# Attention with bias: eight chunks of k or q transposed in one block, and the emission model's cost for it

## The chip, the core and the metric

The kernel runs on one core of a Trainium2 chip. Its engines work from queues of their own, in the order in which the program emits the instructions: TensorE (PE; its weight loads are listed as PEld), VectorE (DVE), ScalarE (ACT), GpSimd (POOL) and SyncE (SP); the last two mostly issue DMAs here. The metric is the device time of one execution in microseconds, lower is better.

## What is computed

Softmax attention with an additive bias that is shared by all batches and heads, for 4 x 8 = 32 heads, 1024 positions and a head dimension of 64, with inputs and outputs in float32:

```python
scale = 1.0 / np.sqrt(head_dim)
scores = scale * np.matmul(q, k.transpose(0, 1, 3, 2))
scores = scores + bias
scores_max = np.max(scores, axis=-1, keepdims=True)
attn = np.exp(scores - scores_max) / (np.sum(np.exp(scores - scores_max), axis=-1, keepdims=True) + 1e-8)
return np.matmul(attn, v)
```

## The kernel before

**Tiling.** Two heads form a pair (16 pairs). The 1024 positions of queries and of keys are cut into 8 chunks of 128. A *slot* is one head with one chunk of queries against all 1024 keys: 256 slots. The scores of a slot, transposed (keys on partitions), fill one of three *places* `pl` in PSUM, each of 128 x 1024 float32 (two banks). The slots are ordered in two groups of pairs (7 and 9). Slots of one chunk of queries follow each other in a place, head after head: only the first of such a chain writes the bias by matmuls (L223), and each later one adds the scores of its head and takes away those of the head before, in one matmul over 64 + 64 rows. So a pair has the operands `ko` and `qo` (both its heads, the first of `qo` negated) for its second head, and `ke` and `qe` for its first, which join it to the second head of the pair before.

**The work of a slot.** Two halves of four matmuls make its *fill* (`fill`, L228; the matmuls are at L226). ScalarE takes the exponential of the place into a tile `E` (L240), of which there are 13. For some slots of place 2, VectorE computes the exponential instead, by a chain of six steps (`d_steps`, L249, lines L257 to L277, tiles `dy`, `df`, `dt`, `de`); which slots these are is decided while the program is emitted, by how much work VectorE has. Then eight matmuls multiply the exponentials by V, with a column of ones for the sum (`av`, L285, matmuls at L294), into a PSUM tile `po` that holds up to seven slots; VectorE divides and copies it out (`evac`, L302 and L304), SyncE stores it.

**Getting k and q ready.** GpSimd's DMAs load k and q of a pair as bf16 with positions on partitions. TensorE transposes them by chunks into a PSUM tile `px` (`transposes`, L164; L173). A chunk takes two transposes, one for each head of the pair, each from 128 x 64 to 64 x 128, placed at its own half of the array's columns by `tile_position`. So eight chunks take 16 instructions on L173. VectorE copies `px` into `ko` or `qo` (`copy_out`, L177, lines L181 and L183). SyncE's DMAs, or VectorE or GpSimd for the first pairs, copy halves of that into `ke` and `qe` (`doubles`, L487; `copy`, L513). `px` and `po` share two PSUM buffers, `xa` and `xb`.

**The order.** The whole program is emitted by hand, in the order that a small model finds while it emits (from about L362 to L796): it keeps a time for each engine (`t_pe`, `t_act`, `t_dve`, ...) and, step by step, emits the candidate that can start first. It runs once, when the program is built; on the chip each engine then follows that fixed order and waits on semaphores. The model's durations are constants in ns: `FILL` 452 for a fill, `AVG` 247 or `AV` 264 for a slot's product with V, `EXP` 906 for an exponential on ScalarE, `TR` 60 for a chunk's transposes, `L_PE`, `L_ACT`, `L_DVE` for the way of a result from an engine to the next.

`pe_cands` (L552) lists what TensorE could do next: a fill for each place (priority 0), a product with V (priority 1), and the next *piece* of transposes, all eight chunks of a pair's k or q, or 3 or 5 of them for the q of the first pairs (priority 2, or 0.5 when the first slot that needs it is nine or fewer ahead). There are 32 such pieces. A piece may start only if few exponentials wait for their product (`lag < 4`), or its first use is less than eight slots ahead.

Before the change a piece is two candidates, one after the other: `begin` emits the first half of its chunks, `end` the rest and queues the copy-out. `half_done` holds the piece that is begun, with its buffer; the second half is free of the condition on `lag`. Between the two other candidates may be emitted, or none.

`pe_pick` (L710) chooses. If a fill can start now, it is taken, unless an urgent candidate fits ahead of the moment at which ScalarE runs out of filled places (`act_free`, L523, less `FILL` and `L_PE`). If no fill can start, another candidate is taken if it ends before a limit worked out from the same moment:

```python
limit = max(min(r), act_free() - FILL - L_PE - MARGIN)
ok = [x for x in others if x[0] + x[1] <= limit]
```

Of the kernel before, what the change touches and what calls it, by code (L numbers as in the profile page):

```python
# [16 lines left out]
def kernel(  # L17
# [143 lines left out]
    def linked(pr):  # L161
        return pr + 1 < NP

    def transposes(pr, which, c0, n, tag, px=None, at=0, to=None):  # L164
        if px is None:
            px = ps_x.tile([P, n, P], BF, tag=tag, name="px")
        for c in range(at, to or n):
            if (pr, which, c0) in raws:
                nc.tensor.transpose(px[:, c, :], raws[pr, which, c0][:, c].rearrange("p t d -> p (t d)"), ident[:])
                continue  # L170

            for t in range(2):
                nc.tensor.transpose(px[t * D:(t + 1) * D, c, :], lands[pr, which][:, t, c + c0 * (pr > 0), :], ident[:],  # L173
                                    tile_position=(0, t * D))
        return px
# [141 lines left out]
    with tc.manual_schedule():  # L317
# [68 lines left out]
        t_pe, t_act, t_dve, t_pool = 9300.0, 9900.0, 9600.0, 12800  # L386
# [3 lines left out]
        x_free = {"xa": T0, "xb": T0}  # L390
# [16 lines left out]
        next_fill, next_act = 1, 1  # L407
# [3 lines left out]
        dve_q = []  # L411

        b_tag, closed = [], []
        TR = 60
        LAG, AVG = 7, 247
        half_done = []
        free_lands, loads, loads_v = set(), list(range(EARLY, NP)), []
        sp_q, t_sp = [], T0
        AHEAD, SLACK = 60, 300
# [112 lines left out]
        def fill_ready(s):  # L532
            p = before[s]
            t = 0.0
            if p is not None:
                if p in used:
                    t = used[p]
                elif p in filled and p not in dslots:
                    t = act_free(p) + L_ACT
                else:  # L540
                    return None
            for key in keys(s):
                if get(key) is None:
                    return None
                t = max(t, get(key))
            if slots[s][3]:
                if slots[s][1] not in bias_at:
                    return None
                t = max(t, bias_at[slots[s][1]])
            return t  # L550

        def pe_cands():  # L552

            out = []
            for x in range(3):
                if not queue[x] or queue[x][0] > next_fill + WINDOW:
                    continue
                s = queue[x][0]
                r = fill_ready(s)
                if r is not None and (before[s] is None or before[s] in used):  # L560
                    cost = FILL + BIAS * bool(slots[s][3] and s > 1)

                    def do(t, s=s, x=x, cost=cost):
                        nonlocal next_fill
                        fill(s)
                        filled[s] = t + cost + L_PE
                        queue[x].pop(0)
                        next_fill = min([y[0] for y in queue.values() if y], default=NS)
                        if may_d[s] and backlog(t) < ROOM and len(open_d) < 3:
                            dslots.add(s)  # L570
                            avq.remove(s)
                            start_d(s)
                        else:
                            acts.append(s)
                    out.append((max(t_pe, r), cost, do, 0, s))


            todo = []
            if avq:
                group = [s for s in avq[:1] if round_of[s] == round_of[avq[0]]]  # L580
                have = [s for s in group if s in e_at]
                lag = len([s for s in avq[:NE] if s in e_at])
                if len(have) < len(group):
                    group = have if lag >= LAG and have[:1] == avq[:1] else []
                if avq[0] >= NS - 3:
                    group = [s for s in avq[:1] if s in e_at]
                if group and all(slots[s][2] // 2 in v_at for s in group):
                    todo.append((max(max(e_at[s], v_at[slots[s][2] // 2]) for s in group), group))
            if dav:
                todo.append((dav[0][0], [dav[0][1]]))  # L590
            if todo:
                r, group = min(todo)
                b = len(closed)
                if b_tag:
                    tag = b_tag[0]
                    group = group[:7 - len(bank[b][1])]
                else:
                    f, tag = min((x_free[y], y) for y in x_free)
                    r = max(r, f)
                cost = AVG * len(group) if len(group) > 1 else AV  # L600
                if r < 1e11:
                    def do(t, group=group, b=b, tag=tag, cost=cost):
                        b_tag[:] = [tag]
                        x_free[tag] = 1e12
                        av(group, b, tag)
                        for s in group:
                            if s in dslots:
                                dav.pop(0)
                            else:
                                avq.remove(s)  # L610
                            av_done[s] = t + cost
                        next_v(t)
                        n = len(bank[b][1])
                        if n == 7 or n == 6 and not (dav and dav[0][0] < t + cost + 600) or len(av_done) in (NS - 1, NS):
                            closed.append(b)
                            b_tag.clear()
                            close(b, tag, t + cost + L_PE)
                    out.append((max(t_pe, r), cost, do, 1, 0))
            if pieces:
                pr, which, c0, n = pieces[0]  # L620
                need = need_at[pr, which, c0]
                ring = pr + linked(pr) - RING
                lag = len([s for s in avq[:NE] if s in e_at])
                if ((pr, which, c0) in raw_at and next_fill >= need - AHEAD and (ring < 0 or last_slot[ring] < next_fill)
                        and (lag < 4 or need - next_fill < 8 or half_done)):
                    f, tag = half_done[0] if half_done else min((x_free[y], y) for y in x_free)
                    r = max(f, raw_at[pr, which, c0])
                    to = n if half_done else (n + 1) // 2
                    cost = (n // 2 if half_done else to) * TR
                    urgent = need - next_fill < 12  # L630
                    if r < 1e11:
                        def begin(t, pr=pr, which=which, c0=c0, n=n, tag=tag, to=to):
                            px = transposes(pr, which, c0, n, tag, to=to)
                            x_free[tag] = 1e12
                            half_done[:] = [(t, tag), px, to]

                        def end(t, pr=pr, which=which, c0=c0, n=n, tag=tag, cost=cost):
                            pieces.pop(0)
                            px = transposes(pr, which, c0, n, tag, px=half_done[1], at=half_done[2])
                            half_done.clear()  # L640
                            if pr < EARLY and which == 0 and c0 + n == NCH:
                                freed(pr, t)

                            def run(t2):
                                copy_out(pr, which, c0, n, px)
                                done = t2 + 60 * n + (180 if which else 300)
                                x_free[tag] = done + L_DVE
                                if which:
                                    ready["ko", pr] = done + L_DVE
                                else:  # L650
                                    ready["qo", pr, c0] = done + L_DVE
                                doubles(pr, which, c0, n, done, urgent)
                            dve_q.append((t + cost + L_PE, 0 if urgent else 2, 60 * n + (180 if which else 300), run))
                        out.append((max(t_pe, r), cost, end if half_done else begin, 2 if next_fill < need - 9 else 0.5, 0))
            return out

        def pool(at, cost=0):
# [94 lines left out]
        while next_fill < NS or next_act < len(acts) or avq or dav or dve_q or sp_q:  # L752
            c = []
            if next_act < len(acts):
# [4 lines left out]
                if next_act < NE or acts[next_act - NE] in av_done:  # L759
                    r = max(t_act, filled[s], av_done[acts[next_act - NE]] if next_act >= NE else 0)  # L760
# [13 lines left out]
            t, who = min(c)  # L774
# [14 lines left out]
            else:  # L789
                t_pe = t + p[1]  # L790
# [31 lines left out]
```

## Time and profile before

| | |
|---|---|
| median of 3 runs | 238.88 us (238.15 to 239.96) |
| the profiled execution | 238.87 us, its span 236.8 us |
| TensorE busy / weight loads | 227.0 us (96%) / 211.0 us (89%) |
| ScalarE busy | 222.9 us (94%), 237 exponentials |
| VectorE busy | 197.8 us (84%), 20 exponentials by its chain |
| GpSimd busy | 50.1 us (21%) |
| transposes on L173 | 490, from 10.8 to 141.8 us |
| granted TensorE clock | 0.998 |

Matmuls are pipelined: an instruction is listed for longer than the distance to the next (219 ns for one of a fill, of which eight start within 0.45 us), so busy shares of TensorE overstate how full it is; the distance from the start of one group to that of the next says more. The same holds, less strongly, for ScalarE: an exponential is listed with 1.07 us. The time outside the span (2.07 us) is part of the device time. In rows of the timeline the columns are start and length in us, engine, line, operation, output and input with shapes, the number of instructions merged into the row, and in brackets the idle time before it with what ended it.

### The profile page before, as it was taken

What the parts mean: (1) busy time and instruction counts of PE and PEld (TensorE: products, weight loads), DVE (VectorE), ACT (ScalarE), POOL (GpSimd) and SP (SyncE); (2) the same over time, 40 slices, a digit from 0 to 9 for tenths busy, and PEclk for the clock granted to TensorE, in tenths of its full rate; (3) what the DMA queues carried; (4) which work ended last, traced back from release to release, by engine and by line L of the source; (5) the groups of instructions that cost most, each with busy time, mean ns of one, the idle gap of its engine ahead of it and who ended that gap; (6) DMA issues with size and microseconds to landing.
All of it is one profiled execution on the core that took longest, in us unless ns stands there. A gap on an engine that the chain in (4) does not pass through costs nothing.

```text
span 236.8 us, 10752 instructions
## 1 busy us (share of the span) xinstructions
PE 227.0 (96%) x4743; PEld 211.0 (89%) x4743; DVE 197.8 (84%) x287; ACT 222.9 (94%) x241; POOL 50.1 (21%) x72
## 2 busy tenths in 40 slices
PE   7989999999999999999999999999999999999992
PEld 2879988899989999999999889999999999999981
DVE  2575585889989999989889988998999999899961
ACT  4699998999999999999999999999999999999993
POOL 8844417556403202206131000000000000000000
PEclk9999999999999999999999999999999999999999
DMA  6999999999995948596989452111111111211212
GB/s 210 205 204 214 225 226 210 203 193 204 200 208 122 155 113 156 118 217 97 159 187 183 114 136 64 36 42 42 42 43 44 39 44 47 55 50 49 67 42 61
DMA packets 55358, 29.76 MB, mean 126 GB/s; under 512 B 30800, under 2 KB 51664, under 8 KB 55312
## 3 DMA queue, kind: packets, MB, share of 16 engines
q0 software_dynamic: 30336, 14.06, 47.2%
q1 hardware_dynamic: 24832, 14.50, 23.7%
q8 instruction: 37, 0.61, 1.1%
q10 hardware_dynamic: 144, 0.52, 0.8%
q14 instruction: 9, 0.07, 0.1%
HBM read 29.36 MB, written 8.39 MB: 159 GB/s over the span
## 4 chain that ended last, share of the span: by engine, by line
PE 69%; ACT 16%; issue 7%; DMA 4%; POOL 3%; ACTq 1%; DVE 0%; POOLq 0%
PE pl L226 39%; PE po L294 20%; ACT E L240 16%; PE px L173 7%; DMA q<-in_q_dram 4%; PE pl L223 2%; ACTq L817 1%; POOL k L130 1%; POOL braw L336 0%; POOL qz L332 0%; POOL qs L333 0%; POOL q L138 0%; POOL v L145 0%; POOL ident masks.py:199 0%; DVE ob L304 0%
## 5 line engine op out<-in xcount | busy, mean ns | idle before, releaser
L240 ACT ACTIVATE E<-pl 128x1024 bf16<-128x1024 f32 (+1 forms) x237 | 219.8, 1068 | 6.0 <-PE pl L226 4.9
L294 PE MATMUL po<-vall,E 128*128 128x65 bf16 x1888 | 92.3, 194 | 1.9 <-ACT E L240 1.0
L294 PEld LDWEIGHTS <-E 128*128 128x128 bf16 x1888 | 77.6, 98 | 2.8 <-ACT E L240 1.4
L226 PE MATMUL pl<-qo,ko 128*128 128x128 bf16 x1024 | 77.3, 219 | 0.9 <-ACT E L240 0.2
L226 PEld LDWEIGHTS <-ko 128*128 128x128 bf16 x1160 | 69.0, 98 | 5.3 <-issue 1.0
L226 PE MATMUL pl<-qe,ke 128*128 128x128 bf16 x888 | 66.3, 219 | 1.6 <-DVE qe L194 0.6
L226 PEld LDWEIGHTS <-ke 128*128 128x128 bf16 x888 | 52.6, 98 | 5.1 <-issue 1.0
L257 DVE TENSOR_SCALAR dy<-pl 128x1024 int32<-128x1024 f32 x20 | 24.4, 1221 | 3.7 <-PE pl L226 3.5
L304 DVE TENSOR_TENSOR ob<-po,rs 128x448 f32<-128x448 f32 (+3 forms) x40 | 23.4, 585 | 1.5
L277 DVE SCALAR_TENSOR_TENSOR de<-dy,dt 128x1024 uint16<-128x1024 int32 x20 | 24.4, 1218 | 0.0
L266 DVE SCALAR_TENSOR_TENSOR dt<-df 128x1024 f32<-128x1024 f32 x20 | 24.3, 1217 | 0.0
L272 DVE SCALAR_TENSOR_TENSOR dt<-df,dt 128x1024 f32<-128x1024 f32 x20 | 24.3, 1217 | 0.0
L269 DVE SCALAR_TENSOR_TENSOR df<-dt,df 128x1024 f32<-128x1024 f32 x20 | 24.3, 1217 | 0.1
L138 POOL DMA_DIRECT2D q<-in_q_dram x16 | 11.5, 719 | 42.9 <-PE pl L226 33.0
L149 POOL DMA_DIRECT2D vall<-in_v_dram x18 | 16.2, 907 | 11.7 <-PE pl L226 8.7
L181 DVE COPY ko<-px 128x1024 bf16<-128x1024 bf16 (+1 forms) x16 | 10.8, 673 | 8.5 <-PE px L173 8.0
L302 DVE RECIPROCAL rs<-po 128x7 f32<-128x7 f32 (+3 forms) x40 | 7.9, 197 | 11.8 <-PE po L294 11.4
L183 DVE TENSOR_SCALAR qo<-px,sgn 128x1024 bf16<-128x1024 bf16 (+2 forms) x18 | 12.4, 690 | 5.0 <-PE px L173 4.9
L262 DVE TENSOR_SCALAR df<-dy 128x1024 f32<-128x1024 uint16 x20 | 13.7, 690 | 0.0
L223 PE MATMUL pl<-ident,braw 128*128 128x128 bf16 x136 | 11.7, 228 | 0.3 <-issue 0.2
L130 POOL DMA_DIRECT2D k<-in_k_dram x15 | 10.7, 714 | 3.2 <-PE px L173 1.8
L173 PE MATMUL px<-ident,q 128*64 128x128 bf16 x240 | 11.0, 223 | 0.1
(50 smaller groups left out, 105.9 us busy)
## 6 DMA issues: line engine op xcount, KB each, us to landing
k<-in_k_dram POOLq DMA_DIRECT2D x15, 256.0 KB, 9.6
q<-in_q_dram POOLq DMA_DIRECT2D x14, 256.0 KB, 9.4
out_dram<-ob SPq DMA_DIRECT2D x50, 64.0 KB, 1.8
out_dram<-ob SPq DMA_DIRECT2D x31, 96.0 KB, 3.5
ke<-ko SPq DMA_DIRECT2D x22, 128.0 KB, 5.6
vall<-in_v_dram POOLq DMA_DIRECT2D x18, 128.0 KB, 7.8
qe<-q SPq DMA_DIRECT2D x17, 128.0 KB, 4.2
out_dram<-ob SPq DMA_DIRECT2D x63, 32.0 KB, 1.6
```

The lines of the kernel that those rows point to most:

```text
L149: nc.gpsimd.dma_start(out=vall[:, (2 * pr + t) % VR, :, :D], in_=vf[pr, :, t])
L173: nc.tensor.transpose(px[t * D:(t + 1) * D, c, :], lands[pr, which][:, t, c + c0 * (pr > 0), :], ident[:], tile_position=(0, t * D))
L223: nc.tensor.matmul(to, braw[:, c, :].rearrange("p (kp kc) -> p kc kp", kc=NCH)[:, kc, :], ident8[:], start=i == 0, stop=False, skip_group_ ...
L226: nc.tensor.matmul(to, kk[:, kc, :], qq[:, c, :], start=False, stop=True, skip_group_check=True)
L240: nc.scalar.activation(e[:, i:i + n].rearrange("p b x -> p (b x)"), places[slots[s][0]][:, i:i + n].rearrange("p b x -> p (b x)"), ACTF.Ex ...
L257: w.tensor_scalar(t["y"][:], places[slots[s][0]].rearrange("p b x -> p (b x)"), scale * LOG2E * 65536.0, 127.0 * 65536.0, op0=ALU.mult, op ...
L266: w.scalar_tensor_tensor(t["t"][:], t["f"][:], -G, t["f"][:], op0=ALU.add, op1=ALU.mult)
L269: w.scalar_tensor_tensor(t["f"][:], t["t"][:], Q, t["f"][:], op0=ALU.mult, op1=ALU.add)
L272: w.scalar_tensor_tensor(t["t"][:], t["f"][:], V, t["t"][:], op0=ALU.add, op1=ALU.mult)
L277: w.scalar_tensor_tensor(etile[s].bitcast(U16).rearrange("p c q -> p (c q)"), t["y"][:], 1.0 / 512.0, t["t"][:], op0=ALU.mult, op1=ALU.add)
L294: nc.tensor.matmul(po[:, j + i, :], etile[s][:, kc, :], vall[:, slots[s][2] % VR, kc, :], start=j + i + kc == 0, stop=kc == NCH - 1, skip_ ...
L304: nc.vector.tensor_tensor(ob[:, :n, :], po[:, :n, :D], rs[:, :n, :].to_broadcast([P, n, D]), op=ALU.mult)
```

## The change

The argument range of `transposes` goes; all chunks of a piece are emitted by one call. `begin` and `end` become one candidate, `do`, so nothing is emitted between the chunks of a piece, and `half_done` and the exception that it made from the condition on `lag` go with it. The modelled cost of a piece of n chunks becomes n x 56 + 190 ns; before, it was 60 ns for each chunk of a half. The copy-out is queued at the modelled end of the block, as before. All else in the model and in the emitted work is as it was; as the model's times change, the order and the choice of the slots that VectorE takes are found anew.

```diff
@@ -161,10 +161,10 @@
     def linked(pr):
         return pr + 1 < NP
 
-    def transposes(pr, which, c0, n, tag, px=None, at=0, to=None):
+    def transposes(pr, which, c0, n, tag, px=None):
         if px is None:
             px = ps_x.tile([P, n, P], BF, tag=tag, name="px")
-        for c in range(at, to or n):
+        for c in range(n):
             if (pr, which, c0) in raws:
                 nc.tensor.transpose(px[:, c, :], raws[pr, which, c0][:, c].rearrange("p t d -> p (t d)"), ident[:])
                 continue
@@ -411,9 +411,8 @@
         dve_q = []
 
         b_tag, closed = [], []
-        TR = 60
+        TR, SWITCH = 56, 190
         LAG, AVG = 7, 247
-        half_done = []
         free_lands, loads, loads_v = set(), list(range(EARLY, NP)), []
         sp_q, t_sp = [], T0
         AHEAD, SLACK = 60, 300
@@ -622,22 +621,16 @@
                 ring = pr + linked(pr) - RING
                 lag = len([s for s in avq[:NE] if s in e_at])
                 if ((pr, which, c0) in raw_at and next_fill >= need - AHEAD and (ring < 0 or last_slot[ring] < next_fill)
-                        and (lag < 4 or need - next_fill < 8 or half_done)):
-                    f, tag = half_done[0] if half_done else min((x_free[y], y) for y in x_free)
+                        and (lag < 4 or need - next_fill < 8)):
+                    f, tag = min((x_free[y], y) for y in x_free)
                     r = max(f, raw_at[pr, which, c0])
-                    to = n if half_done else (n + 1) // 2
-                    cost = (n // 2 if half_done else to) * TR
+                    cost = n * TR + SWITCH
                     urgent = need - next_fill < 12
                     if r < 1e11:
-                        def begin(t, pr=pr, which=which, c0=c0, n=n, tag=tag, to=to):
-                            px = transposes(pr, which, c0, n, tag, to=to)
+                        def do(t, pr=pr, which=which, c0=c0, n=n, tag=tag, cost=cost):
                             x_free[tag] = 1e12
-                            half_done[:] = [(t, tag), px, to]
-
-                        def end(t, pr=pr, which=which, c0=c0, n=n, tag=tag, cost=cost):
                             pieces.pop(0)
-                            px = transposes(pr, which, c0, n, tag, px=half_done[1], at=half_done[2])
-                            half_done.clear()
+                            px = transposes(pr, which, c0, n, tag)
                             if pr < EARLY and which == 0 and c0 + n == NCH:
                                 freed(pr, t)
 
@@ -651,7 +644,7 @@
                                     ready["qo", pr, c0] = done + L_DVE
                                 doubles(pr, which, c0, n, done, urgent)
                             dve_q.append((t + cost + L_PE, 0 if urgent else 2, 60 * n + (180 if which else 300), run))
-                        out.append((max(t_pe, r), cost, end if half_done else begin, 2 if next_fill < need - 9 else 0.5, 0))
+                        out.append((max(t_pe, r), cost, do, 2 if next_fill < need - 9 else 0.5, 0))
             return out
 
         def pool(at, cost=0):
```

## The prediction

> **What bounds the kernel now.** I read the chain of waits first, then the waits, ScalarE's timeline, the windows by stage and TensorE's timeline around the transposes.
>
> ```profile
> PE 69%; ACT 16%; issue 7%; DMA 4%; POOL 3%; ACTq 1%; DVE 0%; POOLq 0%
> PE pl L226 39%; PE po L294 20%; ACT E L240 16%; PE px L173 7%; DMA q<-in_q_dram 4%; PE pl L223 2%; ACTq L817 1%; POOL k L130 1%; POOL braw L336 0%; POOL qz L332 0%; POOL qs L333 0%; POOL q L138 0%; POOL v L145 0%; POOL ident masks.py:199 0%; DVE ob L304 0%
> ```
>
> The chain runs through TensorE, with 7% of the span in the transposes (L173). It does not say whether ScalarE has slack, so its timeline comes next: a row is a run of exponentials without a gap over about 0.15 us, and the bracket tells the gap before it.
>
> ```profile
> 22.73 2.85 ACT L240 ACTIVATE E<-pl 128x1024 bf16<-128x1024 f32 x3 [0.18 <-PE pl L226]
> 26.04 11.11 ACT L240 ACTIVATE E<-pl 128x1024 bf16<-128x1024 f32 x12 [0.46 <-PE pl L226]
> ...
> 40.97 2.85 ACT L240 ACTIVATE E<-pl 128x1024 bf16<-128x1024 f32 x3 [0.76 <-PE pl L226]
> 44.04 3.78 ACT L240 ACTIVATE E<-pl 128x1024 bf16<-128x1024 f32 x4 [0.21 <-PE pl L226]
> ...
> 88.68 44.80 ACT L240 ACTIVATE E<-pl 128x1024 bf16<-128x1024 f32 x47 [0.16 <-PE pl L226]
> 133.82 52.02 ACT L240 ACTIVATE E<-pl 128x1024 bf16<-128x1024 f32 x56 [0.34 <-PE pl L226]
> 186.16 46.85 ACT L240 ACTIVATE E<-pl 128x1024 bf16<-128x1024 f32 x51 [0.32 <-PE pl L226]
> ```
>
> The last row gives ScalarE's own pace: (46.85 - 1.07) / 50 = 0.916 us per exponential (one takes 1.07 us, the next begins before it ends). At 88.68 it is (44.80 - 1.07) / 46 = 0.951: small delays that no bracket shows. From 9.12 to 133.82 lie 129 exponentials, one of half size; at 0.916 they need 117.7 us and took 124.7, so ScalarE lost **7.0 us**. From 133.82 to the end of the last at 233.0 it lost 99.2 - (106 x 0.916 + 1.07) = 1.0 us. All transposes lie before 142. So ScalarE sets the end, TensorE starves it in the first 134 us, and a saving on TensorE counts only where ScalarE is late.
>
> Windows by stage (columns PE, PEld, DVE, ACT, POOL busy, then clock, DMA share, GB/s):
>
> ```profile
> 88.00:133.82 45.82, 45.34 (x1000) 42.32 (x1000) 41.65 (x58) 44.74 (x48) 10.81 (x13) 1.00 1.01 155
> 142.00:186.00 44.00, 43.49 (x922) 42.27 (x923) 41.25 (x51) 43.70 (x48) 0.00 (x0) 1.00 0.18 47
> ```
>
> TensorE's busy column is no help: 99% in both. Start to start is better: a fill (8 matmuls, L226) takes 0.445 us where something follows at once, an attention-times-V group (L294) 0.26. Measured so, TensorE is idle for about 0.9 us in all between 80 and 122, outside the transposes: it is full there. Then the transposes:
>
> ```profile
> 86.86 0.61 PE L226 MATMUL pl<-qo,ko 128*128 128x128 bf16 x8
> 87.39 0.64 PE L173 MATMUL px<-ident,k 128*64 128x128 bf16 x16
> 87.97 0.62 PE L226 MATMUL pl<-qe,ke 128*128 128x128 bf16 x8
> ...
> 99.24 0.61 PE L226 MATMUL pl<-qe,ke 128*128 128x128 bf16 x8
> 99.78 0.41 PE L173 MATMUL px<-ident,q 128*64 128x128 bf16 x8
> 100.13 0.62 PE L226 MATMUL pl<-qe,ke 128*128 128x128 bf16 x8
> 100.68 0.41 PE L173 MATMUL px<-ident,q 128*64 128x128 bf16 x8
> 101.03 0.62 PE L226 MATMUL pl<-qo,ko 128*128 128x128 bf16 x8
> ```
>
> A fill ahead of transposes takes 0.54 instead of 0.445: 0.10 is lost on entry. Sixteen transposes take 0.57 to 0.58 to the next fill, but 0.47 where further transposes follow (62.30 to 62.77), so 0.10 is lost on leaving. A whole block costs 0.10 + 0.57 = 0.67, a half 0.10 + 0.35 = 0.45. The Trainium skill, TensorEngine Tiling (Array Packing), Key Properties, says that changing the tiling mode drains TensorE, which names what the two ends are; the sizes are the trace's.
>
> **What the change does, part by part.**
>
> Merged halves. The two halves are separate candidates, yet in 18 places the old order put whole blocks, or several, back to back. Counting rows of L173, 25 blocks of 8 stand alone: 13 pieces were truly split (one first half rides on another block at 62.77). Each merged piece saves 0.90 - 0.67 = 0.23 us of TensorE, 13 x 0.23 = 3.0 us; the joined blocks at 10.84 and 62.30 may come apart, which gives 2 x 0.2 = 0.4 back. Net 2.6 us, the most that merging can give.
>
> How much reaches the end? I took, for each split piece, the lateness of the exponentials that follow its halves (starts beyond 0.916 after the one before), cut at 0.23: pieces at 76.9, 81.8, 99.8, 106.2, 115.9 and 140.4 give 0.23 each, 109.5 gives 0.19, 122.6 gives 0.14, 62.8 gives 0.10, and those at 13.8, 31.3, 89.5 and 137.4 nothing, because ScalarE had work in hand there. Sum **1.8 us**; less 0.1 for the blocks that come apart.
>
> The model's cost. It counted 8 x 60 = 480 ns for a piece and now counts 8 x 56 + 190 = 638; the trace shows 670. Before, each block overran its place in the plan by 0.2. The unsplit blocks show the result: exponentials late by 0.45 (22.7), 0.87 (40.97), 0.33 (44.0), 0.27 (88.7), 0.25 (126.9), 0.11 (130.6), 0.20 (134.9), sum 2.5 us. Cutting 0.19 from each (0.11 from the sixth) would give 1.25. But the work must still be done in a full stage; what can move is an attention-times-V group, which may wait until the thirteen E buffers are used up. Bounds: 0 to 1.25 here. I take 0.4, nearer the lower end, since between 80 and 122 only 0.9 us of TensorE's time is unused. Below zero is possible: a block of 638 must fit ahead of the fill that ScalarE next needs (the limit in `pe_pick`), where 240 fitted sooner; that is the slower rival.
>
> VectorE. `ko` and `qo` copies waited 8.0 and 4.9 us for L173 (waits table), partly because the copy is placed when the model thinks the block is done. In VectorE's queue the approximated exponentials stand behind it. With 638 the copy is placed 0.16 later; no new wait arises, so I count 0. The same for the PSUM buffer of a split piece: it was held across 0.9 to 1.9 us between the halves and is now held less, which only helps the groups that share it. SyncE's `ke`/`qe` copies follow the copy-out; pairs 7 to 15 have due slots ten and more slots (over 8 us) ahead of first use, and those copies land in 4.2 to 5.6 us (median), so they stay hidden; without that cover each would delay a fill. POOL's loads are called as early pairs are freed; at the old ends of split pieces, so 0.
>
> Number of VectorE exponentials: 20 now, chosen by modelled VectorE backlog. Each more or less moves ScalarE by 0.92 us. Modelled TensorE gains 29 pieces of eight chunks x 0.158 and three smaller ones x 0.17 = 5.1 us of work, and one chain takes 6.3 modelled us, so at most one more. I keep 20; the other value goes into the range.
>
> Sum: 1.8 - 0.1 + 0.4 = 2.1 us off the profiled execution's 238.87 (span 236.8 plus 2.07 outside it; the median is 238.88): **236.8 us**.
>
> **Rivals.**
> - *Lateness per piece stays.* Seven late whole blocks of 18 cost 2.5 us, 0.14 a piece; single halves cost about 1.9 over 13 pieces, 0.15 a piece. If a whole block disturbs as now, merging moves 13 x 0.01 = 0.1 us and TensorE's saving turns into idle time: 238.7. For: equal prices. Against: whole blocks were placed by a model 0.19 short, and the dear ones stand before 45 us.
> - *The plan becomes right.* All lateness tied to transposes goes (2.5 + 1.9 = 4.4 us): 234.5; with one more VectorE exponential 233.6. For: TensorE's order is fixed in advance, so an honest price moves groups behind the fills. Against: the full stage at 80 to 122.
> - *Slower.* A whole block stands between two fills, and with a group beside it the distance fill to fill is 0.445 + 0.26 + 0.67 = 1.37 against ScalarE's 0.916; without work in hand ScalarE waits 0.46, as at 22.7 (0.45), and 0.87 where a fill for VectorE comes first (40.97). Nine of the 13 pieces have lateness behind them today, so ScalarE has nothing in hand there; at 0.46 in place of 0.15 each, 9 x 0.31 = 2.8 us are lost: 241.7. It loses from 0.15 a piece upward and passes 1% at 0.15 + 2.4 / 9 = 0.42. For: the early rows; against: three PSUM places and the new cost in the limit. The Trainium skill, Perfetto Trace Analysis, Optimizing Scalar/DVE Operations, says that breaking up instructions may let work be completed sooner if they cause bubbles on other engines; it is said of other engines than TensorE, and the rows at 99.78 and 100.68, each followed by a fill, are what would be given up.
>
> That the block is not contiguous can be ruled out: the changed code emits it in one loop, in TensorE's own order.
>
> **How the numbers follow.** Forecast 0.42, its own range 235.4 to 238.0 (one VectorE exponential and the 0 to 1.25 bound); lateness stays 0.21; plan right 0.21; slower 0.16. The range leaves out a little of each outer case: 234.2 to 240.5. One per cent, about what a measurement of this kernel can tell from no change, is 2.4 us: faster below 236.5, slower above 241.3. Faster takes the 0.21 and 0.18 of the forecast; slower 0.11 of its rival; the rest is 0.50.
>
> **What would show it.** At most 32 blocks on L173 in place of 43, all of 16 or several pieces together (10, 10 and 6 for the divided pairs), 0.67 each: the first step. ScalarE's lost time before 142 down from 7 to near 5 us: the second; unchanged speaks for the first rival, under 3 for the second. Exponentials late by 0.4 and more behind whole blocks after 60 us: the third. A count of `dy` other than 20 shifts all by 0.92 each. A new order that makes a fill wait for `ke` or `qe`, or for a bias row, would make the prediction wrong for a reason outside it.

## The result, and the profile after

The changed kernel takes 241.02 us (median of 18 runs, 238.55 to 243.42), the kernel before 238.47 in runs beside it (237.86 to 240.77): a ratio of **1.0081** (95% interval 1.0055 to 1.0108). The profiled execution took 241.62 us, its span 239.8. A second profile of the same kernel (below) took 242.19, ratio 1.0133 (1.0079 to 1.0186). Ratios are not those of the medians (1.0107 here), and they leave out runs more than 1.5% above the fastest of their kernel: one of 18 here (243.42 us) and three of ten in one experiment.

| | before | after |
|---|---|---|
| rows of transposes on L173 | 43 | 31 |
| exponentials on ScalarE / VectorE | 237 / 20 | 236 / 21 |
| first exponential starts | 8.05 us | 9.16 us |
| ScalarE late, all told | 9.6 us | 12.1 us |
| of that from 100 to 160 us | 2.7 us | 5.9 us |

"Late" adds up, over all exponentials, what the start lies beyond 0.916 us after the start before it; the last row takes those whose start before lies from 100 to 160 us. The rows account for the execution: 2.5 more of lateness, 1.1 more at the start (first loads, which scatter: from 8.0 to 9.4 us in the fourteen traces), 0.92 less for the exponential that went to VectorE: 2.7 us; the last exponential starts 2.6 us later.

ScalarE's timeline of the changed kernel, with the gap before each run of exponentials in brackets:

```profile
75.86 40.23 ACT L240 ACTIVATE E<-pl 128x1024 bf16<-128x1024 f32 x43 [0.83 <-PE pl L226]
117.54 23.94 ACT L240 ACTIVATE E<-pl 128x1024 bf16<-128x1024 f32 x26 [1.44 <-PE pl L226]
142.93 4.69 ACT L240 ACTIVATE E<-pl 128x1024 bf16<-128x1024 f32 x5 [1.46 <-PE pl L226]
149.31 12.16 ACT L240 ACTIVATE E<-pl 128x1024 bf16<-128x1024 f32 x13 [1.69 <-PE pl L226]
...
188.69 46.85 ACT L240 ACTIVATE E<-pl 128x1024 bf16<-128x1024 f32 x51 [0.34 <-PE pl L226]
```

Before, no gap after the first exponential was longer than 0.76. Three of 1.4 to 1.7 us are new, and two of them lie at 143 and 149, where before ScalarE ran from 133.82 to 185.84 without a gap over 0.15. Without their lateness of 1.5 + 1.7 + 1.8, 7.0 of the 12.1 us are left, against 9.6 in all before. The pace of the last row is the old one.

The waits of the changed kernel (total us, times, longest) name what is new:

```profile
ACT E L240 <- PE pl L226: 9.7, 11, 1.7
...
PE pl L226 <- DMA qe<-q: 1.6, 1, 1.6
...
PE px L173 <- issue: 1.3, 1, 1.3
```

A fill waited for the copy of `qe`; before, no fill waited for any DMA. The 1.3 us without a releaser, inside a block of transposes, is the gap at 117.5; it is taken up in the experiments. Where `qe` is late shows in TensorE's transposes. First the kernel before, pairs 13 to 15 (k, q, k, q, k, q; two rows where a piece is split):

```profile
122.57 0.41 PE L173 MATMUL px<-ident,k 128*64 128x128 bf16 x8
123.72 0.41 PE L173 MATMUL px<-ident,k 128*64 128x128 bf16 x8
125.58 0.64 PE L173 MATMUL px<-ident,q 128*64 128x128 bf16 x16
129.34 0.64 PE L173 MATMUL px<-ident,k 128*64 128x128 bf16 x16
133.65 0.64 PE L173 MATMUL px<-ident,q 128*64 128x128 bf16 x16
...
```

The changed kernel, the same pieces up to k of pair 15, after q of pair 12 in the first row:

```profile
120.45 0.64 PE L173 MATMUL px<-ident,q 128*64 128x128 bf16 x16
130.22 0.64 PE L173 MATMUL px<-ident,k 128*64 128x128 bf16 x16
136.85 0.64 PE L173 MATMUL px<-ident,q 128*64 128x128 bf16 x16
138.94 0.64 PE L173 MATMUL px<-ident,k 128*64 128x128 bf16 x16
140.23 0.64 PE L173 MATMUL px<-ident,q 128*64 128x128 bf16 x16
140.70 0.61 PE L173 MATMUL px<-ident,k 128*64 128x128 bf16 x16
```

For ten microseconds no piece goes in; then five come within eleven, three of them with a single fill between. For pairs 7 to 15 the slot by which a piece counts as needed, its *due slot*, is a constant of the program (`DUE`); for pairs 13 to 15 it lies 14, 12 and 10 slots ahead of the first slot that uses the pair. Counted in the order that the programs emit (a split piece at its second half), in slots ahead of the piece's due slot:

| piece | k13 | q13 | k14 | q14 | k15 | q15 |
|---|---|---|---|---|---|---|
| before | 5 | 3 | 7 | 2 | 6 | 3 |
| after | -3 | -10 | -5 | -6 | 2 | -3 |

What a late piece does, in the timeline of the changed kernel (all engines):

```profile
140.23 0.64 PE L173 MATMUL px<-ident,q 128*64 128x128 bf16 x16
...
140.91 0.75 DVE L183 TENSOR_SCALAR qo<-px,sgn 128x1024 bf16<-128x1024 bf16 x1
...
142.18 0.42 DVE L200 TENSOR_SCALAR q<-qo 128x1024 bf16<-128x1024 bf16 x1
...
143.47 1.75 SPq L514 DMA_DIRECT2D ke<-ko  x3
...
145.33 1.96 SPq L514 DMA_DIRECT2D qe<-q  x2
...
148.60 0.61 PE L226 MATMUL pl<-qe,ke 128*128 128x128 bf16 x8 [1.57 <-DMA qe<-q]
```

From the transposes to the fill it is 8.4 us: the copy-out, the negated copy, then SyncE's queue, in which stores and the `ke` copies of the other late pieces stand ahead, then the DMA. TensorE takes its queue in order, so it stands still before that fill, and ScalarE after it. The loss at 142.9 is the same bunching on TensorE: three whole blocks and one fill take 2.4 us (138.94 to 141.3), in which ScalarE does two and a half exponentials, and a group of matmuls with V then waits 0.40 us for VectorE's copy out of `px`.

Why did the model postpone them? A piece may go in if ScalarE has work for its cost and a fill beyond: 638 + 452 + 205 = 1295 ns, where a half asked for 240 + 657 = 897. While k13 waited, ten or eleven of the thirteen `E` tiles were waiting for their group. At eleven the rule in `pe_pick` puts a group first (`short`); at ten the model's lead (how long ScalarE still has work) was 0.68 to 1.28 us, too little, but for two steps (1.40 and 1.54), at which an exponential came first and made it eleven. The piece went in at 1.73. In the kernel before, the halves of k13 went in at leads of 1.08 and 1.03. That is read from the program. The test does not do it alone: the larger charge, by which the model sees TensorE fuller, is needed too, as the emitted orders of two experiments below show. What it costs was put to the chip.

### The profile page after: what moved, and what is told of

The parts are those of the page before. It is cut to its first block, busy times and chain, and to the rows that moved or that the text cites. A ratio compares the mean times of both kernels' runs of the same rounds, so it can differ in the third digit from the quotient of the medians.

```text
span 239.8 us, 10736 instructions
## 1 busy us (share of the span) xinstructions
PE 225.7 (94%) x4743; PEld 211.7 (88%) x4743; DVE 203.6 (85%) x293; ACT 221.0 (92%) x240; POOL 50.0 (21%) x72
## 4 chain that ended last, share of the span: by engine, by line
PE 54%; ACT 25%; issue 11%; DMA 4%; DVE 4%; SPq 1%; DVEq 0%; ACTq 0%
PE pl L226 30%; ACT E L240 25%; PE po L294 15%; PE px L173 6%; PE pl L223 3%; DMA dt<-in_k_dram 2%; DMA qe<-q 1%; DVE ko L181 1%; DMA out_dram<-ob 1%; SPq L661 0%; DVE dt L266 0%; DVE df L269 0%; DVE ob L304 0%; DVE qo L183 0%; DVE de L353 0%
## 5 line engine op out<-in xcount | busy, mean ns | idle before, releaser
L226 PEld LDWEIGHTS <-ko 128*128 128x128 bf16 x1160 | 70.1, 98 | 4.5 <-issue 0.3
L257 DVE TENSOR_SCALAR dy<-pl 128x1024 int32<-128x1024 f32 x21 | 25.6, 1220 | 2.8 <-PE pl L226 2.7
L269 DVE SCALAR_TENSOR_TENSOR df<-dt,df 128x1024 f32<-128x1024 f32 x21 | 25.5, 1217 | 0.1
L266 DVE SCALAR_TENSOR_TENSOR dt<-df 128x1024 f32<-128x1024 f32 x21 | 25.5, 1216 | 0.1
L277 DVE SCALAR_TENSOR_TENSOR de<-dy,dt 128x1024 uint16<-128x1024 int32 x21 | 25.6, 1218 | 0.0
L272 DVE SCALAR_TENSOR_TENSOR dt<-df,dt 128x1024 f32<-128x1024 f32 x21 | 25.5, 1217 | 0.0
L262 DVE TENSOR_SCALAR df<-dy 128x1024 f32<-128x1024 uint16 x21 | 14.3, 687 | 0.0
L223 PE MATMUL pl<-ident,braw 128*128 128x128 bf16 x136 | 12.4, 237 | 0.5 <-issue 0.5
L223 PEld LDWEIGHTS <-braw 128*128 128x128 bf16 x136 | 10.7, 150 | 0.6 <-issue 0.5
```

The source lines that it names most:

```text
L223: nc.tensor.matmul(to, braw[:, c, :].rearrange("p (kp kc) -> p kc kp", kc=NCH)[:, kc, :], ident8[:], start=i == 0, stop=False, skip_group_ ...
L226: nc.tensor.matmul(to, kk[:, kc, :], qq[:, c, :], start=False, stop=True, skip_group_check=True)
L257: w.tensor_scalar(t["y"][:], places[slots[s][0]].rearrange("p b x -> p (b x)"), scale * LOG2E * 65536.0, 127.0 * 65536.0, op0=ALU.mult, op ...
L266: w.scalar_tensor_tensor(t["t"][:], t["f"][:], -G, t["f"][:], op0=ALU.add, op1=ALU.mult)
L269: w.scalar_tensor_tensor(t["f"][:], t["t"][:], Q, t["f"][:], op0=ALU.mult, op1=ALU.add)
L272: w.scalar_tensor_tensor(t["t"][:], t["f"][:], V, t["t"][:], op0=ALU.add, op1=ALU.mult)
```

## The experiments

Three theories were set against each other at first: **A**, the larger cost makes the model postpone pieces, and late `ke` and `qe` stall the fills; **B**, whole blocks starve ScalarE whatever the model counts (the prediction's slower rival); **C**, the long gaps are TensorE's supply of instructions in the profiled run. Each ratio is against runs of the kernel before on the same chip. Edits are to the changed kernel unless the kernel before is named.

### Whole blocks at the old cost

```diff
-        TR, SWITCH = 56, 190
+        TR, SWITCH = 60, 0
```

> The changed kernel with the model's cost of a piece set back to 60 ns a chunk (480 for eight); the block stays whole. In the changed kernel's emitted order the last five pieces stand 3 to 10 slots behind their due slot; here none is more than 1 behind. Theory A (the larger cost makes the model postpone the pieces, and the late ke and qe stall the fills): 236.5 to 238.5 us, no wait of a fill for the DMA of qe, ScalarE's losses of 1.5 us and more between 140 and 150 gone. Theory B (a whole block between two fills starves ScalarE, whatever the model counts): as the changed kernel, 240 to 242. Theory C (the long gaps are TensorE waiting for instructions, by chance of the run): a gap of over 1 us without a releaser somewhere in the transposes, about 240.

236.91 us, ratio 0.9913 (0.9884 to 0.9943). ScalarE's timeline:

```profile
48.25 71.98 ACT L240 ACTIVATE E<-pl 128x1024 bf16<-128x1024 f32 x77 [0.34 <-PE pl L226]
120.40 6.98 ACT L240 ACTIVATE E<-pl 128x1024 bf16<-128x1024 f32 x7 [0.17 <-PE pl L226]
127.73 4.73 ACT L240 ACTIVATE E<-pl 128x1024 bf16<-128x1024 f32 x5 [0.35 <-PE pl L226]
132.64 98.34 ACT L240 ACTIVATE E<-pl 128x1024 bf16<-128x1024 f32 x107 [0.17 <-PE pl L226]
```

From 48 us to the end ScalarE has no gap over 0.35, with every block whole. A holds; B falls as the account of the slowdown. (The five late pieces that the expectation speaks of are five of the last six in the table above; k of pair 15 is ahead.) As it was the fastest order of all, it was run once more:

> The kernel of the first experiment once more (whole blocks at the old cost), in five rounds: four other orders without late pieces came to 0.996 to 1.000 of the kernel before, this one to 0.991. If its gain is its order's own: 236.5 to 237.3, ratio 0.989 to 0.994. If it was a lucky set of runs: 237.7 to 238.5, ratio about 0.997.

237.29 us, 0.9941 (0.9911 to 0.9970), at the edge between the two expectations: a gain of some 0.6 to 0.9%, less than its first set showed.

### Halves at the new cost

In the kernel before:

```diff
-                    cost = (n // 2 if half_done else to) * TR
+                    cost = (n // 2 if half_done else to) * 56 + 190
```

> The kernel before with its two halves kept, but each half counted with the new cost, 56 ns a chunk + 190 (414 for four). Emitted so, the last pieces stand 4 to 9 slots behind their due slot. Theory A: slower than the kernel before, 241 to 246 us, with fills waiting for ke or qe after 130 us. Theory B: within 1% of the kernel before, 237 to 240.5, since no block is whole. Theory C: as B, with gaps at other places.

241.66 us, 1.0119 (1.0048 to 1.0190). A larger cost alone, without one merged piece, makes the kernel about as slow as the whole change did. It is not the same cost: with 414 ns for each half a piece is charged 828, where the change charges 638. Where the late pieces are, TensorE waits for VectorE's `ko`, behind four halves with a single fill among them:

```profile
147.72 0.42 PE L294 MATMUL po<-vall,E 128*128 128x65 bf16 x8 [1.00 <-DVE ko L181]
```

ScalarE's exponential at 149.2 is 2.3 us late. Theory A had expected fills that wait for a copy; by DMA none did here. The loss is that of pieces bunched together, as at 142.9 in the changed kernel. Another loss, 1.7 us before 55.4, follows the last chunks of q of pair 1, two and four slots behind; there a fill waits for VectorE's `dy`.

### Overdue pieces first

```diff
+                must = [x for x in others if x[3] == 0.5 and need_at[pieces[0][:3]] - next_fill < 2 and x[0] <= t_pe]
+                if must:
+                    return must[0]
                 due = [x for x in others if x[3] in ((0.5, 1) if short else (0.5,)) and x[0] <= t_pe]
```

> The changed kernel, cost and whole blocks kept, with one rule added to the choice for TensorE: a piece whose due slot is less than two slots ahead goes ahead of a ready fill. The last six pieces then stand at most at their due slot instead of up to 10 behind; everything to about 85 us is emitted as in the changed kernel. Theory A: the two losses of 1.7 and 1.8 us between 140 and 150 go, some 3 us less than the changed kernel: 237 to 239. Theory B: no better than the changed kernel, 240 to 242, since a whole block now goes in just where ScalarE has no lead. Theory C: 1.5 us less or more, at random.

238.25 us, 0.9974 (0.9940 to 1.0008). With cost and whole blocks as in the change, only the lateness taken away, the slowdown is gone. ScalarE is late by 2.4 us from 100 to 160, where the changed kernel had 5.9.

### Whole blocks in the old order

In the kernel before:

```diff
-        for c in range(at, to or n):
+        for c in range(0 if at == 0 else n, n):
```

> The kernel before with its model, its costs and so its order unchanged; only where the model places the first half of a piece, all eight chunks are emitted, and nothing where it places the second. 13 pieces are merged, which takes 13 x 0.23 = 3.0 us off TensorE. Theory A: merging by itself does no harm, 236 to 238.5 us. Theory B: the whole blocks stand where the model had left room for a half, ScalarE starves more: 239.5 to 242. The prediction's step on merging: 1.8 us less than before, 236.7.

238.21 us, 0.9962 (0.9934 to 0.9990). Merging by itself gains 0.9 us (0.2 to 1.6) by the ratio, half of the 1.8 predicted.

### The changed kernel once more

> The changed kernel once more, nothing altered, for a second profile. Theory A says that the wait of a fill for the DMA of qe near 148 us and the loss near 142 come again, 1 to 2 us each, since the emitted order makes them. Theory C says that the gap without a releaser inside the transposes at 115 us (1.3 us) is TensorE's supply of instructions in that run: it moves or shrinks below 0.7. If A held also for that gap, it would come again at the same place with the same length. Time 239 to 242.5.

Two rows of TensorE's timeline in this second profile:

```profile
114.87 0.64 PE L173 MATMUL px<-ident,k 128*64 128x128 bf16 x16
...
147.77 0.61 PE L226 MATMUL pl<-qe,ke 128*128 128x128 bf16 x8 [2.07 <-DMA qe<-q]
```

The block at 114.87 is in one piece, where the first profile had a gap of 1.31 us in it: that gap belongs to the run (C). The losses at 141.6 (1.7 us) and 148.5 (2.3 us) came again: those belong to the order (A).

### Lateness put back by hand

```diff
-        TR, SWITCH = 56, 190
+        TR, SWITCH = 60, 0
...
-                        and (lag < 4 or need - next_fill < 8)):
+                        and (need - next_fill < -4 if pr >= 13 else lag < 4 or need - next_fill < 8)):
```

> The whole blocks at the old cost (the first experiment, 236.9 us), with the pieces of pairs 13, 14 and 15 held back by hand until they are more than four slots behind their due slot: they stand 5 to 9 behind, like the changed kernel's 3 to 10; the twelve pieces before them stand as in the first experiment, VectorE takes 20 exponentials. Theory A: the late ke and qe alone bring back the loss, 239 to 242, with fills that wait for ke or qe between 135 and 150. Theories B and D: no whole block is added and no cost is charged, so 236.5 to 237.5 as the first experiment.

241.19 us, 1.0104 (1.0068 to 1.0140). At the old cost, with every piece up to q of pair 12 where the fast kernel has it, lateness alone brings the slowdown back: about 4 us over the kernel without it. TensorE and ScalarE where q of pair 15 is used:

```profile
149.23 0.64 PE L173 MATMUL px<-ident,q 128*64 128x128 bf16 x16
...
153.46 1.50 PE L226 MATMUL pl<-qe,ke 128*128 128x128 bf16 x24 [0.78 <-DMA qe<-q]
...
154.16 1.02 ACT L240 ACTIVATE E<-pl 128x1024 bf16<-128x1024 f32 x1 [2.62 <-PE pl L226]
```

The wait is only 0.78 us, ScalarE's gap 2.62: eight groups put ahead of the waiting fill (2.43 us from 150.25) filled TensorE's time, but nothing filled ScalarE's.

The same with `need - next_fill < 0` in place of -4:

> As the kernel that holds the pieces of pairs 13 to 15 back by hand, but only until they are behind their due slot at all: they stand 1, 3, 1, 3, 5 and 7 slots behind (there 6, 8, 5, 6, 6 and 9, which came to 241.2 us). Theory A, by dose: the pair's first slots come ten and more slots after the due slot and a copy takes 4 to 5 us, some five slots, so only the last two pieces should still be felt: between the two, 237.5 to 239.5. If lateness had no threshold, the cost would go with the mean distance, 3.3 of 6.7 slots: about 239.0.

239.05 us, 1.0017 (0.9984 to 1.0050): between the two, as expected, but no answer on whether there is a threshold, as both readings gave about this. In its profile ScalarE is 1.67 us late at 153.5, and no fill waited for a DMA: the model itself puts nine groups (2.49 us) ahead of the fills that need the last piece.

### Charge and fit apart

A new theory D came in here: that the charged cost harms by itself. First the full charge with a looser fit, in `pe_pick`:

```diff
-                if due and act_free() - FILL - L_PE - MARGIN > t_pe + due[0][1]:
+                if due and act_free() - FILL - L_PE - MARGIN > t_pe + (due[0][1] if due[0][3] == 1 else min(due[0][1], 240)):
...
-            ok = [x for x in others if x[0] + x[1] <= limit]
+            ok = [x for x in others if x[0] + (x[1] if x[3] == 1 else min(x[1], 240)) <= limit]
```

> The changed kernel with the full cost still charged to the model's TensorE time (638 ns for eight chunks), but a piece may go in where 240 ns fit ahead of the fill that ScalarE needs next, as a half could before. In the emitted order no piece stands behind its due slot, and VectorE takes 20 exponentials. Theory A, as I now put it (it is the lateness that costs, and the cost makes it only through the test that the block must fit): 236.5 to 238.5, no fill waits for qe, no loss above 1 us after 100. Rival D (the charged cost harms by itself, because the model then sees TensorE full and holds back other work): slower than the kernel before, 239.5 to 242, though no piece is late.

238.83 us, 0.9979 (0.9954 to 1.0005); no fill waits for a DMA. That is just above theory A's range and well below D's. Against D: the full charge does no large harm when no piece is late. Then the other way round, charged with `n * 60` and with 158 ns added to a piece in both tests:

> The other way round: a piece is charged with 480 ns, as at the old cost, but must fit with 638 ahead of the next fill. In the emitted order no piece stands more than 1 slot behind its due slot, 20 exponentials on VectorE. Theory A in its present form (the fit test makes pieces late) does not hold for this order, since nothing is late: 236.5 to 238. Rival D: also 236.5 to 238, since the charge is the old one. Rival B (whole blocks starve ScalarE where the test leaves no room): better than the first experiment, below 236.5, since the test now leaves the room.

239.02 us, outside the 236.5 to 238 that A and D gave, with a wide spread (236.31 to 241.16). The ratio is 0.9960 (0.9917 to 1.0002), or 0.999 by the means of all ten runs. So the time is no clear answer; what the emitted orders of the two kernels show is that neither the charge nor the fit test makes the pieces late alone; the change does both. That the tighter test would beat the first experiment, as B had it, was not seen.

### Earlier still, and a looser test

Whole blocks at the old cost, with the rule for overdue pieces at less than three slots:

> Whole blocks at the old cost, and a piece whose due slot is less than three slots ahead goes ahead of a ready fill. Every piece of pairs 7 to 15 then stands at least 2 slots ahead of its due slot (in the first experiment the last was 1 behind), 20 exponentials on VectorE. Theory A: beyond being in time nothing is to be had from being earlier, so 236.3 to 237.5, as the first experiment. Theory B: blocks forced in ahead of a ready fill starve ScalarE, 238 to 240.

238.41 us, 0.9968 (0.9930 to 1.0006): not the 236.3 to 237.5 of theory A, but in the 238 to 240 that B gave. And the old charge with a test 100 ns looser (380):

> Whole blocks charged with the old 480 ns, which must fit with only 380 ahead of the next fill. All pieces stand at 0 or more slots ahead of their due slot, 20 exponentials on VectorE. Theory A: as the first experiment, 236.3 to 237.8. Theory B: the block overruns the room by 0.29 us (670 against 380) and ScalarE waits the more, 238 to 240.

239.00 us, 1.0000 (0.9965 to 1.0036), in the range that B gave. So among the seven orders without a piece more than one slot late the ratio still runs from 0.991 to 1.000, while the three in which five or six of the last six pieces are 3 to 10 slots late came to 1.008 to 1.013, and the one with four of them to 1.002. What decides within the lower 1% was not settled: blocks that overrun their room may have a part in it, as B has it, but a tighter test did not help. One cause of scatter shows in TensorE's timeline of the kernel with the rule at three slots: a gap of 1.65 us inside a fill, before 120.55, with no releaser; it made one exponential 1.7 us late.

## Why the prediction was wrong

It forecast 236.8 us, in 234.2 to 240.5, with faster by over 1% at 0.39 and slower at 0.11. It came to 241.02 beside 238.47: slower by 0.8% in the ratio (interval 0.55 to 1.08%), within about the 1% that it counted as no change, but outside the range and on the other side.

- **What bounds the kernel** was right: ScalarE's lateness carries the time in every profile, and the part after 160 us hardly moved (1.0 us before, 1.3 after).
- **The price of a block** was right. In the changed kernel the ends cost 0.094 and 0.10, a whole block 0.66 us (27 blocks); there are 31 rows, "at most 32".
- **Merging** was mis-sized: 1.8 us predicted, 0.9 (0.2 to 1.6) measured with the order held. I gave each lateness behind a half to the halves. In the profile with the order held, 0.5 of 9.6 us of lateness went, and an exponential at 88.0 is late by 0.92, where the one at 88.7 was by 0.27 before; whose delay it is, no run separates.
- **The model's cost** is the step that failed. "I take 0.4, nearer the lower end" counted it as a gain. In the changed kernel it is a loss of 3.3 to 4.0 us: 1.0081 against 0.9941 and 0.9913 for whole blocks at the old cost; on the halves alone a larger cost still (828 for a piece) gave 1.0119. The text saw the lever, "a block of 638 must fit ahead of the fill that ScalarE next needs", and then priced it only as disturbance at the block's own place. What it left out is that a piece which does not fit is put off, and puts off the next.
- **The cover for the copies** is where the loss hid. "Pairs 7 to 15 have due slots ten and more slots ... ahead of first use ... so they stay hidden; without that cover each would delay a fill." The cover was counted from the due slot, as if the pieces would meet it. With q14 put in six slots behind, six of its twelve slots were left, the way to its use took 8.4 us, and a fill stood still for 1.6 us, as the sentence's second half says. The other loss, 1.7 us at 142.9, comes from pieces in a bunch, which the prediction does not have; with the 1.8 at 149.3 it makes 3.5 us.
- **The slower rival** had the right side and the wrong mechanism: whole blocks between two fills. With the order held they gain, and the slowdown appears with halves. The Trainium skill's sentence (Perfetto Trace Analysis, Optimizing Scalar/DVE Operations) on breaking up instructions, weighed there, does not carry over to these transposes (0.9962 for whole blocks in the order of the halves); what the small halves were good for is that the model could find room for them.
- **Lateness tied to transposes** fell in part, less than the second rival had it: eight profiles of whole blocks with no piece more than one slot late have 7.4 to 9.1 us of lateness in all, in place of 9.6. VectorE took 21, the other value in the range.

## What to carry to other kernels

A cost in an emission model does two things: it advances the clock, and it decides what may go in. Correcting a price that the trace proves too low can make the plan worse, if the work has deadlines and the rule "only where it fits" has no rule "but in time" beside it; ask of each candidate that grows whether it will still find a place before its first user, and price the copies behind it as if it did not. And test such a change as two: the emitted work in the old order, and the new cost on the old work.

## What the runs showed of the hardware

**Gaps of TensorE without a releaser** lie at the same place in the instruction stream. Counting matmuls and weight loads, the gaps longer than 1.2 us from start to start between 80 and 125 us, one in each of seven of the fourteen traces, stand at 168 to 178 of the count modulo 256 (1.28 to 1.87 us; five of them at 119 to 121 us, the others at 85 and at 115). Two profiles of one program (whole blocks at the old cost) have gaps of 1.56 and 0.73 us at the same count. The trace has an instruction queue of 37 packets of 16 KB, usually some 6 us apart; TensorE's 9486 matmuls and weight loads over 37 are 256 each, so it is taken to be TensorE's. Before the gap at 115 us the packets stood 9.1 us apart. In the second profile of the same kernel there was no such gap there. The Trainium skill, Runtime: NRT & Kernel Launch, Instruction fetch mechanics, says that instructions are refilled in blocks of 16 KiB (256 instructions) and that crossing a boundary is mostly hidden. The period of 256 agrees, and so does "mostly": between 80 and 125 us a trace crosses some eight boundaries, and at most one shows such a gap. That late packets cause the gaps is pointed to, not shown: no run changed them.

**Ends of the transposes**: changing between the 64-column tiles and the full array cost 0.10 us each way in every order.
